# A two-layer decoder trunk: normalisation sums kept in the accumulator's bank, and a new order of all instructions

## The chip, the cores and the metric

The kernel runs on one core of one Trainium2 chip. The metric is the device time of one execution in microseconds (us); a run's time is the median of several executions. The engines are TensorE (PE; its weight loads are listed as PEld), VectorE (DVE), ScalarE (ACT), GpSimd (POOL) and SyncE (SP, which only issues transfers here). Each engine takes its instructions strictly in the order of its own queue and waits at the head of the queue until what the instruction needs is there.

## The reference

256 tokens of width 1024 pass through two layers. Layer 0 mixes with block-sparse attention (16 heads of 64; with 256 tokens there is one block, so it is causal attention), layer 1 with three dilated sliding windows (12 heads). After each mixer comes a dense MLP of width 4096 with a squared ReLU. Each of the four sub-layers ends in the same normalisation:

```python
def layer_norm(x, g, b):
    mu = jnp.mean(xf, axis=-1, keepdims=True)
    var = jnp.mean(jnp.square(xf - mu), axis=-1, keepdims=True)
    y = (xf - mu) * lax.rsqrt(var + LN_EPS)
    return y * g + b
...
h = layer_norm(DEEPNORM_ALPHA * h + mix, ln_mix_g[i], ln_mix_b[i])
h = layer_norm(DEEPNORM_ALPHA * h + sq_relu_mlp(h, mlp_w_in[i], mlp_w_out[i]), ln_mlp_g[i], ln_mlp_b[i])
```

All data are float32. The kernel multiplies in split precision: a number is held as a rounded high part and a low rest, and a product is three matmuls (high by high, high by low, low by high).

## The kernel before

**Tiling.** The 256 tokens are two halves `m` of 128 rows (partitions). A row of 1024 is two halves `n` of 512 columns, and 512 float32 columns are one bank of PSUM. There are eight banks, four tagged `acc` (accumulators) and four tagged `tp` (transposes, scores, products). Weights are loaded as 128x1024 tiles (512 KB) into a ring of 36 buffers tagged `w`; ACT rounds each to its high part (L503) and DVE subtracts to get the low part (L508).

**The order of the work** is written out by hand. The program first lists its operations: every call of `op(...)` makes one with the next number, its engine and what it reads and writes, in the order of the code. The constant `ORDER` then names those numbers in the order in which they are emitted; `(6, 4)` stands for 6, 7, 8, 9. Each engine's queue is what `ORDER` leaves when only that engine's numbers are kept. Buffers and banks are handed out along the same order, with planned times from a table of costs (the second argument of `op`).

**The start.** Eight stages `kt` (class `Stage`) each bring 128 rows of x transposed and six blocks of 128 weight columns, and PE does 18 matmuls of 256 columns for each. A stage's load can be split over two queues. To set the order in which transfers start, a DVE memset into the target stands ahead of some loads:

```python
BEHIND = {(0, 2): 64, (1, 0): 384, (1, 2): 1}
...
if (kt, first) in BEHIND:
    n = BEHIND[kt, first]
    op("DVE", dve(n), lambda c=c: nc.vector.memset(self.raw.t[:, c], 0.0), (), [(self.raw, first)])
self.load(...)
```

The numbers of the first operations:

| number | engine | what it does | needs |
|---|---|---|---|
| 3 to 9 | PE | matmuls of ones, to keep PE going | |
| 10 | SP | load, stage 0: x and one column block, 192 KB | |
| 11, 12 | DVE, ACT queue | memset of 64; load, stage 0: the other blocks, 320 KB | 12 needs 11 |
| 13, 14 | ACT, DVE | high and low part of x, stage 0 | 10 |
| 15, 16 | DVE, DVE | high part (CAST, L505) and low part of the first block | 10 |
| 17 to 20 | ACT, DVE, ACT, DVE | high and low part of the other blocks | 12 |
| 21, 22 | DVE, SP | memset of 384; load, stage 1: x and two blocks, 256 KB | 22 needs 21 |
| 23, 24 | DVE, ACT queue | memset of 1; load, stage 1: four blocks, 256 KB | 24 needs 23 |
| 25, 26 | ACT, DVE | high and low part of x, stage 1 | 22 |
| 27, 28 | DVE, DVE | high and low part of its first two blocks | 22 |
| 29, 30 | ACT, DVE | high and low part of its other four blocks | 24 |
| 31, 32 | SP | two loads of stage 2, 256 KB each | |
| 40, 45, 50, 55, 60 | SP | loads of stages 3 to 7, 512 KB each | 40 needs a POOL copy (39) that needs 12 |
| 66, 68 to 84 | PE | stage 0's matmuls (67: one of ones between them) | |
| 85 to 102 | PE | stage 1's; 85 needs 25 and 27, 89 needs 25 and 29 | |

**A normalisation** (`ln_half`, once for each `m` of each sub-layer but the very last): for both `n`, DVE forms `alpha*z + bank` (`scalar_tensor_tensor`, L883) from the row's old value `z` in SBUF (tiles `tok`, seen as `tok_float`) and the accumulator's bank, into `z`; `bn_stats` (L1191) reads `z`. Then `bn_aggr` (L1127) gives mean and variance, POOL raises the variance to -0.5 (L1128), DVE centres each half (subtract the mean, times g) and scales it (times the root, plus b). PE transposes the result (L1017) into a `tp` bank, and ACT and DVE split it into the next sub-layer's `xs`.

**The very last half** (`ln_last`) does the same in smaller pieces, since the output waits for it: columns 512:768 are finished in the bank `right`, 768:1024 in a bank of their own (`extra`), 0:512 in `left`; each piece's statistics follow as it is done. After `bn_aggr` (3571), 768:1024 is centred and goes to ACT, POOL and ACT's queue; 512:768, 0:320 and 320:512 (`LAST_SPANS`) are each centred and scaled by DVE and stored from SP.

Of the kernel before, what the change touches and what calls it, by code (L numbers as in the profile page):

```python
# [7 lines left out]
F32 = mybir.dt.float32  # L8
# [3 lines left out]
ALU = mybir.AluOpType  # L12

P = 128
S = 256
# [142 lines left out]
class Plan:  # L158
# [278 lines left out]
def tile_trunk(  # L437
# [22 lines left out]
    nc = tc.nc  # L460
    plan = Plan()
    op = plan.op
# [678 lines left out]
    def ln_last(left, right, extra, gb, alpha):  # L1141
# [4 lines left out]
        for bank, c0, n, k in ((right, 512, S, 1), (left, 0, 512, 0)):  # L1146
# [3 lines left out]
            for i in range(c0 // S, (c0 + n) // S):  # L1150
                op("DVE", dve(S), lambda i=i: nc.vector.bn_stats(st.t[:, i, :], z.t[:, i * S : (i + 1) * S]),  # L1151
                   [(z, k)], [(st, i)])
# [637 lines left out]
```

## Time and profile before

| | |
|---|---|
| median of 3 runs | 539.76 us (539.66 to 540.03) |
| the profiled execution | 539.64 us, its span 537.8 us |
| TensorE clock granted | 0.997 |
| PE | 530.5 us busy, 99% of the span, 3148 matmuls |
| DVE | 503.5 us busy, 94% |
| ACT | 375.0 us busy, 70% |
| POOL | 32.4 us busy, 6% |
| read from HBM, mean | 125.24 MB, 235 GB/s |

The span runs from the first to the last instruction; the rest of an execution's time lies around it. In a list by time the columns are start, length, engine, line, operation, out<-in, shape and count, and in square brackets the engine's idle time before it and what ended that. A length of "x2" spans both. Records of matmuls overlap, since they are pipelined: the distance of two starts is what one costs. DVE's records overlap by some 0.07 us where neither waits for the other.

### The profile page before, as it was taken

To read this page: it belongs to the slowest core of one execution; us is meant where nothing else is said; L and a number is where in the kernel's file an instruction comes from. 1 tells how busy PE (TensorE), PEld (TensorE's weight loads), DVE (VectorE), ACT (ScalarE), POOL (GpSimd) and SP (SyncE) were. 2 spreads that over 40 slices of the span, in tenths; PEclk is the share of its full clock that TensorE was granted. 3 is DMA by queue.
4 is the path that set the end of the run, shared out by engine and by line. 5 is a ranking of instruction groups with operands and counts; after the bars stand their busy time and mean duration, and the time that the engine had idled before them with its cause. 6 is when DMAs were issued, how large, how long until landed. Compare 5 with 4: busy or idle time off the path is not lost.

```text
span 537.8 us, 8728 instructions
## 1 busy us (share of the span) xinstructions
PE 530.5 (99%) x3148; PEld 450.8 (84%) x3148; DVE 503.5 (94%) x869; ACT 375.0 (70%) x616; POOL 32.4 (6%) x43
## 2 busy tenths in 40 slices
PE   9999999999999999999999999999999999999995
PEld 7988888888888888888888888878888888888884
DVE  5799999998999999999999899889999999999997
ACT  5469878357978886877806558828788788688811
POOL 0000000011001000000000000001000000000002
PEclk9999999999999999999999999999999999999998
DMA  8999357196889699898685287696798787976302
GB/s 309 417 417 395 101 164 274 57 324 173 253 260 343 176 283 302 215 338 318 221 293 194 79 267 203 187 306 135 213 297 289 217 273 193 347 215 177 129 1 78
DMA packets 38491, 126.86 MB, mean 236 GB/s; under 512 B 4272, under 2 KB 5168, under 8 KB 38448
## 3 DMA queue, kind: packets, MB, share of 16 engines
q1 hardware_dynamic: 34128, 111.43, 57.8%
q0 software_dynamic: 3888, 14.16, 14.5%
q10 hardware_dynamic: 432, 0.72, 0.4%
q8 instruction: 25, 0.41, 0.3%
q14 instruction: 18, 0.15, 0.1%
HBM read 125.24 MB, written 1.05 MB: 235 GB/s over the span
## 4 chain that ended last, share of the span: by engine, by line
PE 98%; DVE 1%; DMA 1%; ACT 0%; POOL 0%; issue 0%; POOLq 0%
PE acc L512 69%; PE tp L512 27%; PE tp L1017 2%; DMA w<-in_xw_dram 1%; DVE tok L883 0%; DVE bst L1151 0%; POOL rstd L1128 0%; ACT tok L1171 0%; ACT xs L503 0%; DVE bst L1154 0%; DVE mv L1127 0%; POOLq L1128 0%
## 5 line engine op out<-in xcount | busy, mean ns | idle before, releaser
L508 DVE TENSOR_TENSOR w<-w_raw,w 128x1024 fp32r<-128x1024 f32 x205 | 243.2, 1218 | 1.3 <-ACT w L503 1.2
L512 PE MATMUL acc<-xs,w 128*128 128x256 f32 (+1 forms) x1264 | 232.6, 331 | 0.1
L512 PEld LDWEIGHTS acc<-xs,w 128*128 128x128 f32 x1264 | 198.6, 189 | 29.2 <-ACT xs L503 0.9
L503 ACT ACTIVATE w<-w_raw 128x1024 fp32r<-128x1024 f32 x205 | 206.9, 1053 | 9.8 <-PE acc L512 7.6
L512 PE MATMUL acc<-w,ahi 128*128 128x512 f32 (+1 forms) x314 | 90.4, 390 | 0.0
L512 PEld LDWEIGHTS acc<-w,ahi 128*128 128x128 f32 x314 | 57.6, 188 | 11.5 <-issue 0.3
L512 PE MATMUL acc<-w,alo 128*128 128x512 f32 (+1 forms) x145 | 49.2, 388 | 0.0
L512 PE MATMUL tp<-w,alo 128*128 128x512 f32 (+1 forms) x175 | 47.4, 389 | 0.0
L797 POOL DMA_DIRECT2D w_raw<-in_wout_dram x27 | 24.0, 889 | 328.1 <-PE acc L512 82.5
L1278 ACT ACTIVATE ta<-acc 128x256 f32<-128x256 f32 x48 | 18.2, 380 | 31.7 <-PE acc L512 31.3
L512 PE MATMUL acc<-w,xs 128*128 128x512 f32 (+1 forms) x168 | 38.7, 365 | 0.0
L876 DVE TENSOR_TENSOR w_raw<-w_raw 128x512 f32<-128x512 f32 x54 | 36.6, 685 | 0.2
L876 DVE TENSOR_TENSOR ta<-acc,ta 128x256 f32<-128x256 f32 x70 | 29.1, 421 | 8.1 <-ACT ta L1278 4.5
L503 ACT ACTIVATE xs<-tp 128x512 fp32r<-128x512 f32 x12 | 7.1, 598 | 42.3 <-PE tp L1017 42.2
L512 PEld LDWEIGHTS tp<-w,alo 128*128 128x128 f32 x175 | 31.7, 188 | 5.6
L512 PE MATMUL tp<-w,xs 128*128 128x512 f32 x120 | 32.6, 394 | 0.0
L512 PEld LDWEIGHTS acc<-w,xs 128*128 128x128 f32 x168 | 27.7, 188 | 4.5 <-issue 0.3
L512 PEld LDWEIGHTS acc<-w,alo 128*128 128x128 f32 x145 | 26.7, 188 | 5.2
L512 PE MATMUL tp<-xs,w 128*128 128x256 f32 (+1 forms) x128 | 27.4, 339 | 0.0
L512 PEld LDWEIGHTS tp<-w,xs 128*128 128x128 f32 x120 | 21.8, 188 | 4.0
L876 DVE TENSOR_TENSOR ta<-ta,ta 128x128 f32<-128x128 f32 (+1 forms) x68 | 24.6, 368 | 0.4
L1000 ACT ACTIVATE w<-w,mx 128x128 f32<-128x128 f32 (+2 forms) x40 | 19.9, 503 | 5.5 <-DVE mx L990 5.4
(132 smaller groups left out, 607.5 us busy)
## 6 DMA issues: line engine op xcount, KB each, us to landing
w_raw<-in_win_dram SPq DMA_DIRECT2D x64, 512.0 KB, 6.7
w_raw<-in_wout_dram SPq DMA_DIRECT2D x64, 512.0 KB, 6.4
w_raw<-in_wout_dram POOLq DMA_DIRECT2D x27, 512.0 KB, 8.0
w_raw<-in_wqk_dram SPq DMA_DIRECT2D x22, 512.0 KB, 7.8
w_raw<-in_wo_dram SPq DMA_DIRECT2D x14, 512.0 KB, 7.7
w_float<-in_wout_dram SPq DMA_DIRECT2D x27, 256.0 KB, 7.0
w_raw<-in_wv_dram SPq DMA_DIRECT2D x8, 512.0 KB, 9.5
w<-in_xw_dram SPq DMA_DIRECT2D x5, 512.0 KB, 7.1
```

What stands on the lines that cost most here:

```text
L503: op("ACT", act(n, sbuf=sbuf), lambda: nc.scalar.activation(hi(), src(), AF.Copy), r, whi)
L508: lambda: nc.vector.tensor_tensor(lo(), src(), f32(hi()), op=ALU.subtract), list(r) + list(whi), wlo,
L512: nc.tensor.matmul(out_ap, lhsT, rhs, start=start, stop=stop)
L797: "POOL", 1.2, lambda: nc.gpsimd.dma_start(x.raw, pair[:, 512:1536], accum_op=ALU.add), xk, xk,
L876: op("DVE", dve(n) + extra, lambda: nc.vector.tensor_tensor(out_ap(), a(), b(), op=alu), r, w)
L1000: lambda: nc.scalar.activation(e(), e(), AF.Exp, bias=bias(), scale=-1.0, accum_out=total()), r, w,
L1017: nc.tensor.transpose(ps.t[:, c : c + P].bitcast(F32R), src(), ident.t)
L1278: op("ACT", act(S), lambda: nc.scalar.activation(h(), ps.t[:, S:], AF.Copy), [ps], [(t, i)])
```

## The change

In `ln_half` the sum is written back into the accumulator's bank; `bn_stats` and the centring read the bank, and the centring writes `z`. A bank is thus held until its centring. In `ln_last` the same is done for 0:512 (`left`); 512:768 stays as it was. The centrings are now 768:1024, 512:768 and one of 0:512; the scalings and stores keep their pieces. The matmuls of `extra` no longer name `left` among what they read. The planned costs of POOL's root and of the centrings are lowered. `ORDER` is a new list; it has one operation less (3587).

```diff
 ORDER = (
-    3, 11, 21, 10, 23, 12, 4, 5, 22, 24, 13, 31, (6, 4), 15, 14, 17, 39, 19, 66, 67, 71, 68, 18, 32, 40, 0, 1, 16, 45,
-    50, 20, 27, 29, 25, 73, 69, 33, 35, 37, 43, 41, 30, 26, 28, 34, 38, 36, 42, 44, 55, 60, 72, 74, 76, 78, 79, 83,
...
+    3, 23, 11, 10, 15, 21, 12, 4, 5, 22, 24, 13, 6, 31, 7, 32, 39, 8, 9, 17, 19, 40, 67, 66, 71, 45, 50, 14, 1, 16, 0,
+    18, 20, 27, 55, 25, 29, 60, 65, 26, 28, 68, 69, 73, 74, 72, 223, 35, 33, 226, 78, 70, 75, 76, 79, 80, 83, 85, 84,
+    34, 36, 30, 277, 86, 89, 77, 351, 90, 91, 81, 92, 97, 274, 98, 103, 82, 87, 95, 88, 104, 280, 93, 41, 37, 43, 354,
...
-        op("POOL", 0.6 if ns == 4 else 0.9, lambda: nc.gpsimd.tensor_tensor(rs.t[:, 1:2], mv.t[:, 1:2], expo.t, op=ALU.pow),
+        op("POOL", 0.6, lambda: nc.gpsimd.tensor_tensor(rs.t[:, 1:2], mv.t[:, 1:2], expo.t, op=ALU.pow),
            [mv, expo], [(rs, 1)])
...
         for bank, c0, n, k in ((right, 512, S, 1), (left, 0, 512, 0)):
-            c = slice(c0, c0 + n)
-            stt(n, 0, lambda c=c: z.t[:, c], lambda c0=c0, n=n: z.half(c0 // 512, F32)[:, :n], lambda: alpha, lambda bank=bank, n=n: bank.t[:, :n],
-                ALU.mult, ALU.add, [(z, k), bank], [(z, k)])
-            for i in range(c0 // S, (c0 + n) // S):
-                op("DVE", dve(S), lambda i=i: nc.vector.bn_stats(st.t[:, i, :], z.t[:, i * S : (i + 1) * S]),
-                   [(z, k)], [(st, i)])
+            here = lambda bank=bank, n=n: bank.t[:, :n]
+            full = (lambda c=slice(c0, c0 + n): z.t[:, c]) if k else here
+            w = (z, k) if k else bank
+            stt(n, 0, full, lambda c0=c0, n=n: z.half(c0 // 512, F32)[:, :n], lambda: alpha, here,
+                ALU.mult, ALU.add, [(z, k), bank], [w])
+            for i in range(n // S):
+                op("DVE", dve(S), lambda i=i, c0=c0, full=full: nc.vector.bn_stats(st.t[:, c0 // S + i, :], full()[:, i * S : (i + 1) * S]),
+                   [w], [(st, c0 // S + i)])
...
-        def centre(c0, n, k, src, r):
+        for bank, c0, n in ((extra, 768, S), (None, 512, S), (left, 0, 512)):
             c = slice(c0, c0 + n)
-            stt(n, 1, lambda: z.t[:, c], src or (lambda: z.t[:, c]), lambda: mv.t[:, 0:1], lambda: g.t[:, c], ALU.subtract, ALU.mult,
-                [r, mv, g], [(z, ("c", c0))])
-
-        centre(768, S, 2, lambda: extra.t[:, :S], extra)
+            src = (lambda bank=bank, n=n: bank.t[:, :n]) if bank else (lambda c=c: z.t[:, c])
+            stt(n, 0, lambda c=c: z.t[:, c], src, lambda: mv.t[:, 0:1], lambda c=c: g.t[:, c],
+                ALU.subtract, ALU.mult, [bank or (z, 1), mv, g], [(z, ("c", c0))])
         for eng, c0, n, k, queue in LAST_SPANS:
...
-                centre(c0, n, k, None, (z, k))
...
     in ln_half:
-            stt(512, 0, zn, zn if (m, n) in halved else lambda c=c: z.t[:, c], lambda: alpha, lambda bank=bank: bank.t,
-                ALU.mult, ALU.add, [(z, n), bank] + prev, [(z, n)])
-            op("DVE", dve(512), lambda n=n: nc.vector.bn_stats(st.t[:, n, :], z.half(n, F32)), [(z, n)], [(st, n)])
+            inside = lambda bank=bank: bank.t
+            stt(512, 0, inside, zn if (m, n) in halved else lambda c=c: z.t[:, c], lambda: alpha, inside,
+                ALU.mult, ALU.add, [(z, n), bank] + prev, [bank])
+            op("DVE", dve(512), lambda n=n, bank=bank: nc.vector.bn_stats(st.t[:, n, :], bank.t), [bank], [(st, n)])
...
-            stt(512, 1, zn, zn, lambda: mv.t[:, 0:1], lambda c=c: g.t[:, c],
-                ALU.subtract, ALU.mult, [(z, n), mv, g], [(z, n)])
+            stt(512, 0, zn, lambda n=n: banks[n].t, lambda: mv.t[:, 0:1], lambda c=c: g.t[:, c],
+                ALU.subtract, ALU.mult, [banks[n], mv, g], [(z, n)])
...
     in out_and_ln:
-                    mm_rows([(extra, c0, S)], item, m, [left])
+                    mm_rows([(extra, c0, S)], item, m)
```

What the two lists leave for the queues at the start:

| queue | before | after |
|---|---|---|
| DVE | 11, 21, 23, 15, 14, 18, 0, 1, 16, 20, 27, 30, 26, 28 | 23, 11, 15, 21, 14, 1, 16, 0, 18, 20, 27, 26, 28, 34 |
| SP | 10, 22, 31, 32, 40, 45, 50, 55, 60, 65 | 10, 22, 31, 32, 40, 45, 50, 55, 60, 65 |
| ACT | 12, 24, 13, 17, 19, 29, 25, 33 | 12, 24, 13, 17, 19, 25, 29, 35 |
| PE | 66, 67, 71, 68, 73, 69, 72, 74, 76, 78, 79, 83, 77, 81, 70, 75, 80, 84, 82, 87, 85, 88 | 67, 66, 71, 68, 69, 73, 74, 72, 78, 70, 75, 76, 79, 80, 83, 85, 84, 86, 89, 77 |

At the end DVE's last operations were, before: the sum of 0:512, its two statistics, 768:1024's statistics, aggregate, centre 768, centre 512, centre 0:320, scale 512, scale 0:320, centre 320:512, scale 320:512. After: the sum, the guard (adds the epsilon, L1134; before it stood further ahead), two statistics, 768:1024's statistics, aggregate, centre 768, centre 512, scale 512, centre 0:512, scale 0:320, scale 320:512. Around the four normalisations PE's queue has the transposes at almost the same places in both lists.

More of the change, by code (lines that the diff above doesn't have):

```diff
@@ L1159, in ln_last @@
                [b], [bank])
-        def centre(c0, n, k, src, r):
+        for bank, c0, n in ((extra, 768, S), (None, 512, S), (left, 0, 512)):
             c = slice(c0, c0 + n)
-            stt(n, 1, lambda: z.t[:, c], src or (lambda: z.t[:, c]), lambda: mv.t[:, 0:1], lambda: g.t[:, c], ALU.subtract, ALU.mult,
-                [r, mv, g], [(z, ("c", c0))])
-        centre(768, S, 2, lambda: extra.t[:, :S], extra)
+            src = (lambda bank=bank, n=n: bank.t[:, :n]) if bank else (lambda c=c: z.t[:, c])
+            stt(n, 0, lambda c=c: z.t[:, c], src, lambda: mv.t[:, 0:1], lambda c=c: g.t[:, c],
+                ALU.subtract, ALU.mult, [bank or (z, 1), mv, g], [(z, ("c", c0))])
         for eng, c0, n, k, queue in LAST_SPANS:
             c, bank = slice(c0, c0 + n), banks[c0 // 512]
-            r, w = [(z, ("c", c0)), (rs, 1)], [(z, ("out", c0))]
+            r, w = [(z, ("c", c0 if k else 0)), (rs, 1)], [(z, ("out", c0))]
             if eng == "POOL":
```

302 rows, old and new, of the table ORDER are left out of this document.

## The prediction

> **What bounds the kernel now.** I read the page first, its busy times and its chain of waits:
>
> ```profile
> PE 530.5 (99%) x3148; PEld 450.8 (84%) x3148; DVE 503.5 (94%) x869; ACT 375.0 (70%) x616; POOL 32.4 (6%) x43
> PE 98%; DVE 1%; DMA 1%; ACT 0%; POOL 0%; issue 0%; POOLq 0%
> ```
>
> Then the busy time of each engine by stage, and what TensorE (PE) waits for:
>
> ```profile
> core 0: us, PE busy (x) PEld busy (x) DVE busy (x) ACT busy (x) POOL busy (x), PEclk, DMA share, GB/s
> 0.00:4.90 4.90, 3.98 (x10) 1.54 (x11) 1.40 (x6) 2.40 (x4) 0.39 (x5) 1.00 0.59 198
> 31.00:531.40 500.40, 500.40 (x2951) 424.58 (x2950) 478.63 (x821) 356.60 (x586) 30.14 (x35) 1.00 0.72 229
> 531.40:537.80 6.40, 0.01 (x1) 0.00 (x0) 3.67 (x10) 0.51 (x1) 1.32 (x3) 0.72 0.35 126
> PE tp L512 <- PEq L1775: 0.8, 1, 0.8
> ```
>
> PE is busy for all 500.40 us of the long stretch and is listed waiting only once, at the very start. The change neither adds nor removes a matmul. What can move the end is therefore only the start, the 6.4 us behind the last matmul, and any new hole in between; VectorE (DVE), idle for 500.40 - 478.63 = 22 us of the long stretch, costs nothing until it makes PE wait.
>
> The sum is made against the profiled execution, 539.64 us with a span of 537.8 (1.8 lie around it). The median of the runs shown is 539.76, 0.12 above it. What a measurement of this kernel can tell from no change is about 0.2%, 1.08 us.
>
> **The start.** The new ORDER puts DVE's operations as 23, 11, 15, 21, 14, where the old one has 11, 21, 23, 15, 14. Number 15 rounds the first weight columns and needs the first load (10). Number 21 is the 384-column memset that load 22 on SP (half of stage 1: x and two column blocks) must wait for. DVE takes its operations in order, so 21 now stands behind a wait for a DMA, load 22 stands behind 21, and every later load on SP stands behind 22.
>
> ```profile
> 0.74 2.72 DMA w<-in_xw_dram
> 0.96 0.38 DVE L566 MEMSET w<- 128x384 f32 x1
> 1.37 0.33 SPq L499 DMA_DIRECT2D w<-in_xw_dram  x1
> 3.49 0.23 DVE L505 CAST w<-w 128x128 fp32r<-128x128 f32 x1 [2.14 <-DMA w<-in_xw_dram]
> 4.67 3.10 PE L512 MATMUL acc<-xs,w 128*128 128x256 f32 x21
> 5.79 0.63 ACT L503 ACTIVATE w<-w 128x512 fp32r<-128x512 f32 x1 [0.76 <-DMA w<-in_xw_dram]
> 6.33 0.71 ACT L503 ACTIVATE xs<-w 128x256 fp32r<-128x256 f32 x2
> w<-in_xw_dram SPq DMA_DIRECT2D x3, 256.0 KB, 4.8
> out_dram<-tok_float SPq DMA_DIRECT2D x2, 256.0 KB, 2.0
> L512 PE MATMUL acc<-xs,w 128*128 128x256 f32 x704 | 107.8, 283 | 0.1
> 14.00:20.00 6.00, 6.00 (x53) 6.00 (x52) 3.79 (x7) 4.26 (x7) 0.00 (x0) 1.00 1.04 415
> ```
>
> Load 22 was issued at 1.37. Now: cast until 3.49 + 0.23 = 3.72, memset until 4.10, issue at about 4.13. How long it then takes, no row shows. The bounds are the two rows of transfers that found their queue empty: 2.0 us (the 256 KB stores) and 2.72 (the first load, 192 KB); with 4.8 the others stood behind each other. By then the ACT queue's loads, which keep the engines going, are nearly through, so I take the middle, 2.4: landing at 6.5, between 6.1 and 6.9.
>
> ScalarE (ACT) then splits stage 1's x, 0.71 us for two, so about 0.42 for one: number 25 ends at 6.95. PE reaches its first matmul of stage 1 (85) as the fourteenth from 4.67 on; 21 take 3.10 less the 0.28 that the last one runs on, 0.14 each, so at 4.67 + 13 x 0.14 = 6.5. It waits some 0.5. Three matmuls later (0.36) number 89 needs ACT's operation 29, which is now queued behind 25 though its data is there earlier than before: 6.5 + 0.31 + 0.63 = 7.5 with what a semaphore takes, against 7.0 + 0.36; another 0.15. In the old order 29 ran at 5.79 ahead of 25 and neither was waited for. Against this stand two small holes of the old start that the reordering of 68 to 78 may close (21 at 0.14 where 53 take 6.00 later, 0.11 each; most of that difference is the slow first three, I count 0.15). Sum: 0.5 + 0.15 - 0.15 = **+0.5**, with the bounds of the landing +0.1 to +0.9. Later loads come half a microsecond later too; they cost nothing, since a stage of 18 matmuls takes PE some 2 us (18 x 0.11) and its 512 KB, at the last row's 415 GB/s, 1.3. That cover gone, each late load would cost its own lateness.
>
> **The end.** Of the last normalisation the new code centres 0:512 in one pass out of the bank instead of 320 and 192 out of SBUF, and two of the statistics read the bank.
>
> ```profile
> 530.01 0.69 DVE L883 SCALAR_TENSOR_TENSOR tok<-tok_float,acc 128x512 f32<-128x512 f32 x1
> 530.74 0.75 DVE L1151 BATCH_NORM_STATS2 bst<-tok 128x6 f32<-128x256 f32 x2
> 531.45 0.43 DVE L1154 BATCH_NORM_STATS2 bst<-tp 128x6 f32<-128x256 f32 x1
> 531.91 0.26 DVE L1127 BATCH_NORM_AGGREGATE mv<-bst 128x2 f32<-128x24 f32 x1
> 532.21 0.48 DVE L883 SCALAR_TENSOR_TENSOR tok<-tp,mv,w 128x256 f32<-128x256 f32 x1
> 532.61 0.94 DVE L883 SCALAR_TENSOR_TENSOR tok<-tok,mv,w 128x256 f32<-128x256 f32 x2
> 533.47 0.93 DVE L883 SCALAR_TENSOR_TENSOR tok<-tok,rstd,tp 128x256 f32<-128x256 f32 x2
> 534.76 0.41 DVE L883 SCALAR_TENSOR_TENSOR tok<-tok,rstd,tp 128x192 f32<-128x192 f32 x1
> 535.20 0.33 SPq L1139 DMA_DIRECT2D out_dram<-tok  x1
> L1134 DVE TENSOR_SCALAR bst<-bst 128x1 f32<-128x1 f32 x8 | 1.2, 145 | 0.2
> L883 DVE SCALAR_TENSOR_TENSOR tok_float<-tok_float,mv,w 128x512 f32<-128x512 f32 x14 | 10.2, 752 | 0.2
> L1151 DVE BATCH_NORM_STATS2 bst<-tok 128x6 f32<-128x256 f32 x3 | 1.2, 419 | 0.0
> ```
>
> From 532.21 to the last store's issue at 535.20 DVE is the path. New order: 256 out of the bank (0.40 to the next start), 256 (0.47, because its own scaling follows at once and waits for its end), scaling 256 (0.39), centring 512 (0.75), scaling 320 (0.46), scaling 192 (0.41), three dependent starts of 0.035: 2.98 against 2.99. The pass saved is eaten by the two waits. Ahead of it, the guard (L1134, 0.145 by itself) moves from under the other half's work to between the bank's sum and its statistics, where the sum's end is waited for anyway: 0.05. Reading PSUM instead of SBUF: 431 against 419 ns for the statistics, 483 against 474 for a centring of 256, so 0.01 each. No row has DVE write a bank; the nearest, the sum's own pass of 0.69 that reads one, gives no reason for a price, and I keep -0.05 to +0.15. Sum **+0.05**.
>
> [...]
>
> **The normalisations in between.** All fourteen half-rows' sums stay in their banks; the same passes run, and 752 ns for a centring that reads a per-row mean stay (PSUM sources did not shorten the 256 one). What can change is the wait for POOL's reciprocal root, and when a bank comes free.
>
> ```profile
> 358.73 1.42 DVE L883 SCALAR_TENSOR_TENSOR tok_float<-tok_float,mv,w 128x512 f32<-128x512 f32 x2
> 358.84 1.06 POOL L1128 TENSOR_TENSOR rstd<-mv,expo 128x1 f32<-128x1 f32 x1 [9.84 <-DVE mv L1127]
> 360.06 0.75 DVE L883 SCALAR_TENSOR_TENSOR tok_float<-tok_float,rstd,w 128x512 f32<-128x512 f32 x1
> 359.33 0.39 PE L512 MATMUL acc<-w,alo 128*128 128x512 f32 x1
> 359.56 0.62 PE L512 MATMUL acc<-w,ahi 128*128 128x512 f32 x2
> 361.83 0.40 PE L512 MATMUL acc<-w,alo 128*128 128x512 f32 x1
> 362.21 0.51 PE L1017 MATMUL tp<-ident,tok_float32r 128*128 128x128 f32 x4
> 275.16 0.78 DVE L883 SCALAR_TENSOR_TENSOR tok_float<-tok_float,mv,w 128x512 f32<-128x512 f32 x1
> 277.18 0.74 DVE L883 SCALAR_TENSOR_TENSOR tok_float<-tok_float,mv,w 128x512 f32<-128x512 f32 x1
> 281.44 4.35 PE L512 MATMUL acc<-w,xs 128*128 128x512 f32 x18
> ```
>
> The root took 1.06 beside centrings with two SBUF inputs. Even so it was done at 359.90 and the scaling began at 360.06, when DVE's second centring let it: 0.5 us less on POOL buys nothing there. The only visible hole at a normalisation is 362.21 - 361.83 = 0.38 where a matmul takes 359.56 - 359.33 = 0.23, so 0.15 us; the order of DVE and PE around it is the same in both lists, so it stays. A bank was free after the sum and is now held until its centring, about 2 us more. Who takes these banks next? At 281.44 matmuls that read x of the same rows, which need both centrings (275.16, 277.18) first. So the hold lies under work that waits for more: nothing. For the thousands of other moves I take **0**, between -0.3 (that hole and a few turns into transposes) and +0.5.
>
> Together +0.55: 540.2 in the profile, 540.3 as a median; I say **540.2**.
>
> **Rivals.**
> *Hidden after all.* Load 22 lands by 6.0 because the ACT queue's loads have left the engines running; the old start's holes close and a root finished sooner fills the hole at 362.21: 539.76 - 0.15 - 0.15 + 0.05 = 539.5. For it: the first load's 2.72 began from rest, load 22 does not. Against: 2.0 us is the shortest transfer of that size, and gives 6.1.
> *Slower.* Load 22 takes as long as the first load and its size difference, 2.9: landing at 7.0. Then PE waits 0.95 + 0.15; with loads 31 and 32 (stage 2) behind it and ACT's queue in order, stage 2 may add 0.3: 541.1. It decides from a landing at 7.0 on.
> *Faster.* A shorter root lets every transposed half go earlier: one hole at each of six places would have to be there at 0.2 us to pass 1.08; the waits of PE list none. 538.6 at most. [...]
> *A hold that bites.* An accumulator bank claimed before its centring stops PE for up to 2 us: 541.8. Against it: the claimants read the same x.
>
> **How the numbers follow.** The forecast 0.50, hidden 0.28, slower by the load 0.12, a hold or another hole 0.05, faster 0.05. The likeliest case alone spans 539.8 to 540.8. To hold 8 in 10 the range takes in the hidden case and the lower part of the slower one: 539.2 to 541.2. Faster by over 0.2% is the last case; slower are the two slower ones; the rest is the same within 0.2%.
>
> **What the changed profile would show.** The 384-column memset behind the CAST, near 3.7, and the second load on SP at about 4.1. PE idle or matmuls with over 0.3 between starts near 6.5 to 7.5. The root at 0.55 everywhere, and PE's long stretch without holes. From the last aggregate to the last store's issue 3.0 us again. I am wrong if load 22 is issued near 1.4, if the span falls below 537, or if a hole stands at a normalisation.

## The result: 543.85 us, slower by 0.7%

The changed kernel takes 543.85 us (542.93 to 544.73, 6 runs) against 539.84 us (539.66 to 540.14, 6 runs) of the kernel before on the same chip: a ratio of 1.0074 with an interval of 1.0063 to 1.0085. Three of the six runs lie near 543.0, at a granted TensorE clock of 0.996 to 0.997, and three near 544.6, at 0.993 to 0.994: the clocks are 0.3% apart, and so are the spans (541.2 and 542.9). Four more runs of the same kernel, later, gave 543.08 (542.89 to 543.48). 543.0, or 0.6% more than before, is what the trace accounts for. The profiled execution took 543.01, its span 541.24 us where that of before was 537.85: 3.39 more.

The page of the changed kernel, its busy times, and what PE waits for:

```profile
PE 530.8 (98%) x3148; PEld 450.9 (83%) x3148; DVE 503.8 (93%) x868; ACT 375.2 (69%) x616; POOL 32.3 (6%) x43
```
```profile
PE acc L523 <- ACT w L514: 1.8, 2, 1.6
PE acc L523 <- ACT xs L514: 0.9, 1, 0.9
PE tp L523 <- PEq L1787: 0.8, 1, 0.8
```

PE's work is the same (530.5 before). New are 2.7 us of waits for ACT's splits, all of them at the start. The long stretch in between is unchanged. To cut it off from the start, count matmuls from `xs` and `w` into an accumulator up to the 144th, since the eight start stages have 144. Both lists put a few of the next operations among the last stage matmuls, so the 144th is a mark of equal work and not one operation: in every kernel here 141 matmuls of 256 columns and two of 512 stand ahead of it. It starts at 22.34 before. Here is the stretch of before, from there to the last accumulating matmul, and then the same stretch of the changed kernel, 2.9 later:

```profile
22.30:529.90 507.60, 507.60 (x2988) 430.75 (x2987) 485.74 (x829) 360.39 (x592) 28.89 (x34) 1.00 0.73 232
```
```profile
25.20:532.80 507.60, 507.60 (x2988) 430.70 (x2988) 485.86 (x828) 361.33 (x594) 28.73 (x34) 1.00 0.72 231
```

Both hold 2988 matmuls in 507.60 us without a hole. So the 3.39 us are the start, +2.91 (the 144th matmul starts at 25.25), and what lies behind the last accumulating matmul, +0.47.

**The start of the changed kernel**, the lists by time of DVE, SP (the issue of load 22), PE and ACT, one behind the other:

```profile
3.25 0.23 DVE L516 CAST w<-w 128x128 fp32r<-128x128 f32 x1 [2.28 <-DMA w<-in_xw_dram]
3.51 0.38 DVE L577 MEMSET w<- 128x384 f32 x1
...
3.91 0.33 SPq L510 DMA_DIRECT2D w<-in_xw_dram  x1
...
4.51 1.94 PE L523 MATMUL acc<-xs,w 128*128 128x256 f32 x13 [0.16 <-ACT w L514]
7.40 3.40 PE L523 MATMUL acc<-xs,w 128*128 128x256 f32 x25 [0.94 <-ACT xs L514]
12.42 1.82 PE L523 MATMUL acc<-xs,w 128*128 128x256 f32 x13 [1.61 <-ACT w L514]
...
6.93 0.42 ACT L514 ACTIVATE xs<-w 128x256 fp32r<-128x256 f32 x1 [2.06 <-DMA w<-in_xw_dram]
...
11.43 0.42 ACT L514 ACTIVATE xs<-w 128x256 fp32r<-128x256 f32 x1 [2.95 <-DMA w<-in_xw_dram]
11.76 1.35 ACT L514 ACTIVATE w<-w 128x512 fp32r<-128x512 f32 x2
```

The memset (21) stands behind the CAST (15), as foretold, and load 22 is issued at 3.91. It lands at 6.84, ACT splits x at 6.93, and PE's first matmul of stage 1 starts at 7.40: the first hole. The second hole ends at 12.42, and it is the larger one. There PE waits for ACT's operation 37 (four of stage 2's six weight blocks, the first of the two at 11.76). Its own load had landed at 9.33, but in the new list ACT has 41 (x of stage 3) ahead of it, and ACT waited 2.95 us for the data of 41: load 40. The issues of load 40, first before, then after (512 KB, and the time from issue to landing in us):

```profile
w<-in_xw_dram SPq DMA_DIRECT2D x1, 512.0 KB, 4.0
```
```profile
w<-in_xw_dram SPq DMA_DIRECT2D x1, 512.0 KB, 6.1
```

It was issued at 4.53 and landed at 8.56 before; now it is issued at 5.24, 0.71 later, and lands at 11.35, 2.79 later. The transfers themselves had become slow. Microsecond by microsecond, with the share of the transfer engines that is busy and the GB/s in the last two columns, first before, then after:

```profile
4.00:5.00 1.00, 1.00 (x3) 0.72 (x4) 0.71 (x2) 0.80 (x2) 0.18 (x1) 1.00 0.96 338
7.00:8.00 1.00, 1.00 (x11) 1.00 (x10) 1.00 (x4) 0.86 (x3) 0.00 (x0) 1.00 0.93 381
8.00:9.00 1.00, 1.00 (x11) 1.00 (x10) 1.00 (x3) 0.42 (x1) 0.00 (x0) 1.00 0.88 315
```
```profile
4.00:5.00 1.00, 0.84 (x5) 0.49 (x5) 0.89 (x6) 0.83 (x2) 0.78 (x2) 1.00 0.39 96
7.00:8.00 1.00, 0.60 (x4) 0.49 (x4) 0.85 (x3) 1.00 (x3) 0.00 (x0) 1.00 1.05 182
8.00:9.00 1.00, 1.00 (x10) 1.00 (x10) 0.62 (x3) 0.49 (x2) 0.00 (x0) 1.00 0.96 139
```

From 4 to 5 us the engines run nearly dry (a share of 0.39). From 7 to 9 us they are as busy as before (1.05 and 0.96) and move less than half of what they moved then. The last section says which packets that comes from.

**The end of the changed kernel**, DVE's list, and then one piece of the chain that ended last:

```profile
532.42 0.74 DVE L894 SCALAR_TENSOR_TENSOR tok_float<-tok_float,rstd,w 128x512 f32<-128x512 f32 x1
533.08 0.69 DVE L894 SCALAR_TENSOR_TENSOR acc<-tok_float,acc 128x512 f32<-128x512 f32 x1
...
534.93 0.26 DVE L1138 BATCH_NORM_AGGREGATE mv<-bst 128x2 f32<-128x24 f32 x1
...
535.63 0.48 DVE L894 SCALAR_TENSOR_TENSOR tok<-tok,mv,w 128x256 f32<-128x256 f32 x1
536.24 0.48 DVE L894 SCALAR_TENSOR_TENSOR tok<-tok,rstd,tp 128x256 f32<-128x256 f32 x1
536.64 0.74 DVE L894 SCALAR_TENSOR_TENSOR tok<-acc,mv,w 128x512 f32<-128x512 f32 x1
537.42 0.87 DVE L894 SCALAR_TENSOR_TENSOR tok<-tok,rstd,tp 128x320 f32<-128x320 f32 x2
```
```profile
536.14 0.05 DVEq L894
```

The last bank was done at 532.90, but the sum starts at 533.08: the new list leaves the scaling of the other half until then (532.42), and DVE, not PE, sets the start of the end. That is 0.18 where it was 0.035. Between the centring of 512:768 and its own scaling (536.24 - 535.63 = 0.61 from start to start) DVE stands still for 0.13, part of it on its sequencer (the piece of 0.05 at 536.14). The working of the end follows below.

### The profile page after: what moved, and what is told of

Same layout as the page of the kernel before. It is cut to its first block, busy times and chain, and to the rows that moved or that the text cites. A ratio compares the mean times of both kernels' runs of the same rounds, so it can differ in the third digit from the quotient of the medians.

```text
span 541.2 us, 8757 instructions
## 1 busy us (share of the span) xinstructions
PE 530.8 (98%) x3148; PEld 450.9 (83%) x3148; DVE 503.8 (93%) x868; ACT 375.2 (69%) x616; POOL 32.3 (6%) x43
## 3 DMA queue, kind: packets, MB, share of 16 engines
HBM read 125.24 MB, written 1.05 MB: 233 GB/s over the span
## 5 line engine op out<-in xcount | busy, mean ns | idle before, releaser
L514 ACT ACTIVATE w<-w_raw 128x1024 fp32r<-128x1024 f32 x205 | 209.6, 1054 | 15.6 <-PE acc L523 7.5
L523 PEld LDWEIGHTS acc<-w,ahi 128*128 128x128 f32 x314 | 57.6, 188 | 11.5 <-issue 0.3
L523 PE MATMUL tp<-xs,w 128*128 128x512 f32 (+1 forms) x128 | 27.5, 337 | 0.0
```

What stands on the lines that cost most here:

```text
L514: op("ACT", act(n, sbuf=sbuf), lambda: nc.scalar.activation(hi(), src(), AF.Copy), r, whi)
L523: nc.tensor.matmul(out_ap, lhsT, rhs, start=start, stop=stop)
```

## Experiments

Times of the kernel before in the groups of runs below lie between 539.57 and 539.85. All starts and landings named are read from the profiled execution of each kernel, from its span's start.

### The swap undone, and the swap alone

The changed kernel with 21 ahead of 15 again:

```diff
-    3, 23, 11, 10, 15, 21, 12, 4, 5, 22, 24, 13, 6, 31, 7, 32, 39, ...
+    3, 23, 11, 10, 21, 15, 12, 4, 5, 22, 24, 13, 6, 31, 7, 32, 39, ...
```

> The changed kernel with one move in ORDER: DVE's memset 21 ahead of the CAST 15 again, so that load 22 is issued near 1.4 us; all else as in the changed kernel. Theory 1 (that swap alone makes the whole loss of 4 us): PE has no hole between 5 and 13 us, 539.4 to 540.2. Theory 2 (the rest of the new order, such as ACT's 25 ahead of 29 and PE's early 85, or the banks held longer, bears over 1 us of it): 541 or more, with holes that stay.

540.33 us (539.91 to 540.61), ratio 1.0010 (1.0000 to 1.0019). Load 40 lands at 8.74, the 144th matmul starts at 22.64: 2.6 of the 2.91 us are gone. Without the swap the new list's start costs 0.30 us; the end's 0.47 stays, and the time is a little above theory 1's range.

The kernel before with the swap alone:

```diff
-    3, 11, 21, 10, 23, 12, 4, 5, 22, 24, 13, 31, (6, 4), 15, 14, 17, 39, ...
+    3, 23, 11, 10, 15, 21, 12, 4, 5, 22, 24, 13, 31, (6, 4), 14, 17, 39, ...
```

> The kernel before with the same swap alone (DVE 23, 11, 15, 21, 14; all else in the old order). Theory 1: 543 to 544.5 with the same two holes near 6.5 and 10.5 us. Theory 2: the old order of ACT and PE is more tolerant of the late load: 540.3 to 541.5.

541.48 us (541.33 to 541.60), ratio 1.0030 (1.0018 to 1.0042): at the upper edge of theory 2's range, and far below theory 1's. Load 22 is issued at 3.85 and load 40 lands at 11.38, just as late as in the changed kernel, yet the start is only 1.97 longer (24.31). So the swap makes the late landing, and something else in the new list makes it dearer.

### The code alone, and the order alone

The changed code emitted in the old list's order, and the old code in the new one (the old code's one operation more, the centring of 320:512, behind the scaling of 0:320). The code alone:

```diff
-    3, 23, 11, 10, 15, 21, 12, 4, 5, 22, 24, 13, 6, 31, 7, 32, 39, ...
+    3, 11, 21, 10, 23, 12, 4, 5, 22, 24, 13, 31, (6, 4), 15, 14, 17, 39, ...
```

> The changed code (sums kept in the bank, one centring of 512, no read of left) with the old ORDER carried over number by number. Theory 1: 539.8, within 0.4 of before. Theory 2, banks held longer: 541 or more, with PE idle near a normalisation.

539.92 us (539.58 to 540.34), ratio 1.0005 (0.9995 to 1.0014). The code is neutral: the banks held longer cost nothing, and passes that read or write a bank take as long as ever (a centring out of the bank 746 ns, 752 out of SBUF before; a sum into it 692, 683 before).

```diff
-    3, 11, 21, 10, 23, 12, 4, 5, 22, 24, 13, 31, (6, 4), 15, 14, 17, 39, ...
+    3, 23, 11, 10, 15, 21, 12, 4, 5, 22, 24, 13, 6, 31, 7, 32, 39, ...
```

> The code before with the new ORDER carried over. Theory 1: like the changed kernel, 542.9 to 544.8. Theory 2, if the code bears a part: under 542.

543.49 us (543.42 to 545.18), ratio 1.0076 (1.0060 to 1.0091). The order alone makes the whole loss: its 144th matmul starts at 25.32. Its end shows what the one pass of 512 is worth in this list (DVE's list of the order alone):

```profile
536.62 0.94 DVE L896 SCALAR_TENSOR_TENSOR tok<-tok,mv,w 128x320 f32<-128x320 f32 x1
537.60 0.55 DVE L896 SCALAR_TENSOR_TENSOR tok<-tok,rstd,tp 128x320 f32<-128x320 f32 x1
538.06 0.41 DVE L896 SCALAR_TENSOR_TENSOR tok<-tok,mv,w 128x192 f32<-128x192 f32 x1
538.51 0.41 DVE L896 SCALAR_TENSOR_TENSOR tok<-tok,rstd,tp 128x192 f32<-128x192 f32 x1
```

With two centrings it is 3.77 from the aggregate's end to the last store's issue, with one 3.22. Of these 0.55 us, 0.39 is the pass of 320 itself: 0.94 here, 0.54 in the kernel before. Here it ran beside POOL's addition for 768:1024 (536.49 to 537.21), which before began only when that pass was nearly done. The pass of 512 out of the bank kept its 0.74 beside the same addition. That the addition slows the other pass is a guess: no run here tried it alone. In the old list it is 3.03 with two and 2.89 with one (code alone); there the last store then took 2.04 to land instead of 1.75, with the stores closer together, and nothing was won.

### Operation 37 ahead of 41

```diff
-    ... 104, 280, 93, 41, 37, 43, 354, ...
+    ... 104, 280, 93, 37, 41, 43, 354, ...
```

> The changed kernel with one move on ACT: 37 (rounds stage 2's other weight blocks) ahead of 41 (stage 3's x, which waits for load 40). Theory 1a (the second hole, 1.9 us near 10.5, is 37 standing behind 41 though its own load landed 2 us earlier): the hole falls to about 0.9 as in b_cast_first, the profiled span from 541.2 to about 540.3, 1 us faster than the changed kernel in the same group of runs. Theory 1b (the hole is stage 3's late landing itself): the hole moves but its size stays, 543.

542.34 us (541.92 to 542.45), ratio 1.0045 (1.0030 to 1.0060). Load 40 lands at 11.35 again; the wait of 1.61 at the second hole is down to 0.28 there, with 0.47 at the next place, and the start ends at 24.72, 0.53 earlier, about half of what theory 1a expected. The blocking in ACT's queue is real and is a part of the loss.

### Loads 31 and 32 ahead of 22

They need no memset, so the engines should not run dry while SP waits for 21.

```diff
-    ... 12, 4, 5, 22, 24, 13, 6, 31, 7, 32, 39, ...
+    ... 12, 4, 5, 31, 32, 22, 24, 13, 6, 7, 39, ...
```

> The changed kernel with loads 31 and 32 (stage 2, which wait for nothing) issued on SP ahead of load 22. If the loss is that the transfers ran dry from 4.2 to 5.2 us and every later load stands behind that: no dry spell, 32 lands near 6, 40 near 8.7, the second hole goes, the first (stage 1's x is needed from load 22) stays at 0.5 to 1.3: 540.5 to 541.5. If load 22's own lateness is the whole matter: 542.5 or more.

541.74 us (541.65 to 542.01), ratio 1.0037 (1.0023 to 1.0050). This lies between what the two cases expected. The slow stretch of the changed kernel, now in this one:

```profile
7.00:8.00 1.00, 0.01 (x1) 0.02 (x1) 0.33 (x2) 0.48 (x2) 0.00 (x0) 1.00 1.02 416
8.00:9.00 1.00, 1.00 (x7) 0.89 (x8) 0.73 (x2) 1.00 (x4) 0.00 (x0) 1.00 1.03 397
```

The engines keep their rate: load 40 lands at 8.68 and the second hole is gone. Load 22 now lands behind two others, at 7.43, and the first hole takes its place (PE starts stage 1 at 7.99 instead of 7.40). The start ends at 23.95, 1.6 over before; 1.28 of it is PE's wait for the x of stage 1, which load 22 brings.

### The memset written five times, and three times

The kernel before with 23 first and memset 21 repeated, so that load 22 leaves late though nothing waits for a DMA in front of it:

```diff
+    times = 5 if (kt, first) == (1, 0) else 1
-    op("DVE", dve(n), lambda c=c: nc.vector.memset(self.raw.t[:, c], 0.0), (), [(self.raw, first)])
+    op("DVE", dve(n), lambda c=c, times=times: [nc.vector.memset(self.raw.t[:, c], 0.0) for _ in range(times)], ...
```

> The kernel before with DVE's 23 first and the memset 21 written five times over, so that load 22 is issued near 2.9 us instead of 1.4, without anything waiting for a DMA. If what costs is only the run dry after 4.2 us: the load joins a queue that is still busy and the time stays within 0.4 of before, 539.8 to 540.2. If each microsecond of a late issue costs its share of the 1.7 us of b_cast_first: 540.7 or more.

541.12 us (540.69 to 541.67), ratio 1.0024 (1.0013 to 1.0035). The repeated memsets still took 0.38 us each, but started 0.525 apart, 0.145 behind the end of the one before; so load 22 left at 3.50 instead of the 2.9 meant. It behaves like the swap alone: load 40 lands at 11.46, the start ends at 24.39 (11.38 and 24.31 there). A late issue is enough; the wait for the CAST matters only for the time that it takes.

> The kernel before with 23 first and the memset 21 written three times, nothing else: load 22 should be issued near 2.4 us, between the 1.37 of before and the 3.50 of five memsets. Theory 1 (a late issue costs only once the engines have run out of other transfers, after which packets stay slow): at 2.4 the first loads still run, so the share of the transfers does not fall below 0.5 after 4 us, load 40 lands by 9.2 and the time is within 0.5 of before (539.5 to 540.4). Theory 2 (every bit of lateness of load 22 is paid, in proportion: 1.3 us for a delay of 2.1): 0.6 us slower, 540.3 to 540.7, load 40 landing near 10.

540.74 us (540.11 to 541.01), ratio 1.0017 (1.0007 to 1.0026). Load 22 left at 2.45 and landed at 5.91, early enough for stage 1. What PE waits for in this kernel, and its list:

```profile
PE acc L514 <- ACT xs L505: 0.5, 1, 0.5
PE acc L514 <- ACT w L505: 0.2, 1, 0.2
```
```profile
4.50 6.34 PE L514 MATMUL acc<-xs,w 128*128 128x256 f32 x47 [0.19 <-ACT w L505]
11.36 2.90 PE L514 MATMUL acc<-xs,w 128*128 128x256 f32 x22 [0.51 <-ACT xs L505]
```

The trace accounts for 0.7 of the 1.05 us; the profiled execution itself took 540.37. PE does 47 matmuls in a row, and then waits 0.51 for stage 3's x: load 40, issued at 4.36 (earlier than before), landed at 10.13, 1.57 later than before. The busy share of the engines never fell below 0.72 here, so theory 1's condition, that a late issue costs only once the engines have run dry, falls. Theory 2 is nearer: the later load 22, the larger the loss (0.71 at the start here, 2.05 with five memsets), and it comes through the later loads.

### The two places and the end together

The changed kernel with 21 ahead of 15, 37 ahead of 41, and the centring of 0:512 (3577) ahead of the scaling of 512:768 (3581):

```diff
-    3, 23, 11, 10, 15, 21, 12, ... 93, 41, 37, 43, ... 3576, 3578, 3581, 3579, 3577, 3582, 3580, (3583, 4),
+    3, 23, 11, 10, 21, 15, 12, ... 93, 37, 41, 43, ... 3576, 3578, 3577, 3581, 3579, 3582, 3580, (3583, 4),
```

> The changed kernel with three moves: DVE's 21 ahead of 15, ACT's 37 ahead of 41, and at the end DVE's centring of 0:512 ahead of the scaling of 512:768, which then does not wait for POOL's root. Theory 1: the start as in a_memset_first (+0.3) and the end 0.2 to 0.4 shorter than there: 539.7 to 540.1. If the end's +0.5 has another cause (the spacing of the last two stores): 540.3.

540.18 us (539.58 to 540.37), ratio 1.0004 (0.9995 to 1.0014): the same as before, and between what the two theories expected. Start 22.49. Its end (DVE's list) has no gap left:

```profile
533.33 0.74 DVE L896 SCALAR_TENSOR_TENSOR tok<-acc,mv,w 128x512 f32<-128x512 f32 x1
533.99 1.25 DVE L896 SCALAR_TENSOR_TENSOR tok<-tok,rstd,tp 128x256 f32<-128x256 f32 x3
```

The last store is issued 2.89 behind the aggregate's end, but takes 2.09 to land. From the last accumulating matmul's end to the span's end it is 8.17 us against 8.34 with 21 alone moved, less of a gain than the 0.2 to 0.4 expected. None of the versions tried is measurably faster than the kernel before.

### The changed kernel again, without an edit

> The changed kernel unchanged, for its own spread: both groups of its runs (near 543.0 and near 544.6) should come back if they are two outcomes of the same start; 543.0 alone if the second group belonged to the chip that it ran on. With the start 2.9 longer and the end 0.5 longer, 543.0 to 543.3 is what the traces account for.

543.08 us (542.89 to 543.48), ratio 1.0061 (1.0046 to 1.0076). All four lie near 543.0, at a granted clock of 0.996 to 0.997.

### Where the rest of the start comes from

Two more, both with load 22 still late. The first has 37 ahead of 41 and, on PE, stage 0's last four matmuls ahead of stage 1's first:

```diff
-    ... 80, 83, 85, 84, 34, 36, 30, 277, 86, 89, 77, 351, 90, 91, 81, 92, 97, 274, 98, 103, 82, 87, ... 93, 41, 37, 43,
+    ... 80, 83, 84, 77, 81, 82, 85, 34, 36, 30, 277, 86, 89, 351, (90, 3), 97, 274, 98, 103, 87, ... 93, 37, 41, 43,
```

> The changed kernel with two queue places of the old list back and load 22 still late: on ACT 37 ahead of 41, on PE stage 0's last four matmuls (84, 77, 81, 82) ahead of stage 1's first (85). Load 40 should land near 11.3 again. Theory (the new list doubles what the late load costs, because its ACT and PE queues put work that needs late data ahead of work that doesn't): the hole at 85 shrinks by four matmuls, 4 x 0.11 = 0.45, the 144th stage matmul comes at 24.3 as with the old list and the same late load (24.31), against 24.72 with the ACT change alone; time 541.7 to 542.1. Rival (the difference lies elsewhere in the new list): the hole only moves behind the four matmuls, the 144th stays at 24.7, 542.2 to 542.5.

542.43 us (541.99 to 542.57), ratio 1.0048 (1.0031 to 1.0064). The rival was right: PE's list, with the first hole closed, waits the longer at stage 3:

```profile
4.58 7.35 PE L525 MATMUL acc<-xs,w 128*128 128x256 f32 x50 [0.22 <-ACT w L516]
12.85 0.85 PE L525 MATMUL acc<-xs,w 128*128 128x256 f32 x5 [0.93 <-ACT w L516]
14.19 0.98 PE L525 MATMUL acc<-xs,w 128*128 128x256 f32 x6 [0.48 <-DVE xs L521]
```

Set beside each other, the starts say why. In each kernel whose load 40 comes late, the 144th matmul follows its landing at a fixed distance, whatever holes stand ahead:

| kernel | order of stage 3's splits | load 40 lands | 144th matmul | between |
|---|---|---|---|---|
| three memsets | old | 10.13 | 23.05 | 12.92 |
| swap alone | old | 11.38 | 24.31 | 12.93 |
| five memsets | old | 11.46 | 24.39 | 12.92 |
| 37 ahead of 41 | 37, 41, 43; 44, 42 | 11.35 | 24.72 | 13.37 |
| the same and PE | 37, 41, 43; 44, 42 | 11.57 | 24.95 | 13.38 |
| changed kernel | 41, 37, 43; 44, 42 | 11.35 | 25.25 | 13.90 |
| the same again | 41, 37, 43; 44, 42 | 11.46 | 25.35 | 13.89 |
| order alone | 41, 37, 43; 44, 42 | 11.41 | 25.32 | 13.91 |

The last run gave the changed kernel the old order of these splits, and nothing else:

```diff
-    ... 104, 280, 93, 41, 37, 43, 354, ...  395, 38, 44, 42, 100, ...
+    ... 104, 280, 93, 37, 43, 41, 354, ...  395, 38, 42, 44, 100, ...
```

> The changed kernel with load 22 still late and stage 3's splits in the order of the old list: on ACT 37, 43, 41 (weights' high part, then x's) where the new list has 41, 37, 43; on DVE 42 ahead of 44 (x's low part, then the weights'). Theory: the start ends a fixed time behind the landing of load 40, whatever holes stand ahead of it; that time is 13.9 with the new list (25.25 - 11.35), 13.37 with 37 ahead of 41, and 12.92 with the old list (24.31 - 11.38 with the same late load), and the order of the splits is the whole difference. The 144th stage matmul should come 12.9 to 13.0 behind the landing, near 24.3, and PE no longer wait for a low part of x; time 541.7 to 542.0. Rival (PE's own order in stage 3 makes the rest): 13.4 behind the landing again, near 24.7, time 542.2 to 542.5.

542.22 us (541.99 to 542.31), ratio 1.0047 (1.0030 to 1.0064). The 144th matmul starts at 24.61, 12.95 behind a landing at 11.66, and PE waits for x's high parts alone:

```profile
PE acc L525 <- ACT xs L516: 1.6, 2, 1.0
```

The theory holds in the distance; the time lies at the rival's lower edge because load 40 landed 0.3 later than in the changed kernel.

The table also gives load 40's slack. In the kernel before, the 144th matmul came 13.78 behind its landing (22.34 - 8.56), where the same order needs 12.93: it could land 0.85 later for nothing. The changed start adds up from this: 2.79 of lateness, less 0.85 of slack, plus 0.97 for the new order of the splits (13.90 - 12.93), is 2.91.

## Why the prediction was wrong

It said 540.2 us, from +0.5 at the start, 0 in between and +0.05 at the end. Measured in the profiled execution: +2.91, 0 and +0.47.

**The start: the mechanism was right, its price was not.** The memset behind the CAST near 3.7, load 22 issued late, the ACT split, the wait at PE's matmul 85: all there.

- *The landing of load 22.* Foretold 6.5, with bounds of 6.1 and 6.9; measured 6.84. That it lies inside is luck: the load took 2.93 from its issue, longer than both rows that were to bound it (2.0 and 2.72), but it was issued at 3.91 where 4.13 was counted. The wait at 85 is 0.94 by PE's list where 0.5 was counted. This alone would still have left the time in the range.
- *The later loads: the step that failed.* "... they cost nothing, since a stage of 18 matmuls takes PE some 2 us ... and its 512 KB, at the last row's 415 GB/s, 1.3." The rate was taken from 14 to 20 us, and the engines did not keep it: 96 GB/s from 4 to 5 us, when they ran nearly dry, then 182 and 139 at a busy share of 1.05 and 0.96. Half a microsecond of lateness in the issue (0.71 for load 40) became 2.79 in the landing, against a slack of 0.85. With three memsets load 22 landed in time for stage 1 and the later loads still cost 0.7 us at the start (23.05 against 22.34). The sentence behind it, "That cover gone, each late load would cost its own lateness", comes near what happened; the forecast gave it nothing, and the slower rival 0.3 for stage 2.
- *The order behind the late load.* Not seen at all: ACT's 41, 37, 43 and DVE's 44, 42 put waiting work ahead of ready work and weights ahead of the x that PE needs first. It made 13.90 - 12.93 = 0.97 of the start, 0.53 of it 37 behind 41 and 0.45 the order of x and weights. With load 40 landing early the same order costs little: with 21 ahead of 15 the new list's start ended at 22.64.
- *The slower rival* had this place and direction, but decided from a landing of load 22 at 7.0 on and ended at 541.1. The landing was 6.84, and the loss was reached by load 40.

**In between** the forecast of 0 holds: 507.60 us in both. Centrings and sums in or out of a bank cost what they did in SBUF (groups by line, x14, x11, x10; busy us, mean ns; first before, then after):

```profile
L883 DVE SCALAR_TENSOR_TENSOR tok_float<-tok_float,acc 128x512 f32<-128x512 f32 x10 | 6.8, 683 | 0.8 <-PE acc L512 0.6
```
```profile
L894 DVE SCALAR_TENSOR_TENSOR tok_float<-acc,mv,w 128x512 f32<-128x512 f32 x14 | 10.2, 744 | 0.1
L894 DVE SCALAR_TENSOR_TENSOR acc<-tok_float,acc 128x512 f32<-128x512 f32 x11 | 7.6, 691 | 0.7 <-PE acc L523 0.4
```

744 ns for a centring out of the bank against 752 out of SBUF, 691 for a sum into it against 683. The bank's longer hold stopped nobody.

**The root** was foretold at 0.55 everywhere, which is what six of its eight passes took in the kernel before (0.55 to 0.56, the other two 1.06). Seven of the eight are; one is not (POOL's operations by line, then DVE's list at that place):

```profile
L1139 POOL TENSOR_TENSOR rstd<-mv,expo x8: 547/558/1427, 109.1 to 535.3; 128x1 f32<-128x1 f32 x8
```
```profile
277.70 1.17 DVE L519 TENSOR_TENSOR w<-w_raw,w 128x1024 fp32r<-128x1024 f32 x1
```

At 277.87 the root took 1.43, beside a DVE pass of 1.17 with two SBUF inputs that the new order put next to it. That the pass beside it made it longer is not shown: in the kernel before, of the five roots that began beside a centring with two SBUF inputs, two took 1.06, but three took 0.55 to 0.56 (one of them began at 113.70). With the code alone all eight took 0.55 to 0.56. As forecast, the root moved no time: PE waits nowhere near it.

**The end** came to +0.47 instead of +0.05: the sum starts 0.15 later behind the bank, since DVE was still scaling; from the sum to the aggregate's end 0.05 less; from there to the last store's issue 3.22 where it was 3.03; 0.05 for the landing and 0.12 behind it. The last 0.12 does not always come with this end (behind the landing it is 0.90 before, 1.02 in the changed kernel, but 0.89 in the version with 37 ahead of 41); its cause is open. The prediction summed from the first centring's start and had 2.98 against 2.99; measured were 3.19. Half of the difference is the centring of 512:768, whose scaling follows at once. It counted 0.47 and a dependent start of 0.035 for that, and it took 0.61. A scaling that waits only for the centring just ahead does start 0.04 behind its end (536.64 + 0.74 to 537.42); here a piece of 0.05 on DVE's sequencer stood ahead. This scaling reads POOL's root and a bank that ACT wrote too (`tok<-tok,rstd,tp`), and that the piece comes from those two waits is a guess. The root was not late: it was done at 535.89. The other half lies at SP: it was still issuing the store before until 538.32, and the last one went out 0.13 behind its scaling's end (538.29), where it had been 0.03. And the prediction took DVE to be free when the last bank is done.

## What to carry to other kernels

When a transfer at the head of a queue is made later, look at what lands behind it: set the lateness of each later load against its slack, not only that of the first, and don't take a transfer rate from another stage of the kernel (415 GB/s from 14 to 20 us before, 139 from 8 to 9 us in the changed kernel). Here a start limited by a late load ended at a fixed distance behind that landing (12.92 to 12.95 with the old order of stage 3's splits, 13.89 to 13.91 with the new one), so holes ahead of it were free, and what decided was the order of the splits that waited for it: work whose data is there goes ahead of work that waits (0.53 us here), and what the next engine needs first goes first (0.45). Before a memset is moved behind a wait on its engine, name every queue behind that memset.

## What was not expected of the hardware

Transfers lost more than half their rate while the engines were as busy as ever: 139 GB/s at a share of 0.96 (8 to 9 us) against 315 at 0.88 in the kernel before. The single packets in the traces show that this is not a general slowness. Between 4 and 11.5 us the common packet takes the same in both kernels, 0.084 us for 2 KB and 0.159 for 4 KB. But in the changed kernel ten packets of 4 KB, started between 7.27 and 8.29, took 1.4 to 1.7 us each; load 40 is the first load with rows of 4 KB, and these are among its first. In the kernel before none took over 1 us. The share counts a packet as busy for as long as it takes, and comes to 1.05 from 7 to 8 us at 182 GB/s.

It came in every kernel whose load 22 left at 2.45 or later with the loads of stages 2 and 3 behind it. Take the packets of over 0.25 us in that stretch and add up what they took above the common time: 12 to 26 us of engine time in these kernels, 2 to 5 in the five with load 22 on time or with loads 31 and 32 ahead of it. It does not simply grow with the lateness (12.1 with load 22 at 2.45, 25.9 at 3.91, but 14.5 in the last run, at 3.89), and running dry is not needed for it (three memsets). What makes these packets wait was not found.
